# Two of four column blocks of the gates, pool output and conv output computed with the weights at rest

## The chip, the cores and the metric

One core of a Trainium2 chip runs the kernel. The metric is the device time of one execution in microseconds, lower is better. TensorE (PE) multiplies; its weight loads are shown apart as PEld. VectorE is DVE, ScalarE is ACT, GpSimd is POOL, and SyncE (SP) issues most transfers. Each engine works off its own list in the order in which the program wrote it.

## The reference

256 tokens and 16 meta tokens with 2048 features go through one layer. What the change touches:

```
u    = RMSNorm(h)
proj = u @ w_in          # z_pool 1024 | v 1024 | g 1024 | gate_a 2048 | gate_b 2048
y_a  = pool(z_pool) @ w_pool_out                  # 1024 -> 2048
y_b  = silu(LayerNorm(dwconv31(v * sigmoid(g)))) @ w_conv_out   # 1024 -> 2048
m    = sigmoid(gate_a) * y_a + sigmoid(gate_b) * y_b
h    = h + RMSNorm(m @ w_o)
...  # MLP with relu squared, 2048 -> 8192 -> 2048
```

All is float32.

## The kernel before

**Numbers.** Each float32 operand of a product is split into a high part (rounded to fp32r) and a low part (the rest), and a product is the sum of three: high by high, high by low, low by high. ScalarE makes the high part of a weight chunk (L279), VectorE subtracts it for the low part (L282).

**Chunks.** The weights come as chunks of 1 MB, 128 partitions by 2048 elements, in the order of the list `stream`. `fetch()` (L337) hands out the next chunk. Before that it opens the chunk two further on (its DMA goes to SP's queue), puts that chunk's split into the lists of ScalarE and VectorE, and calls `flush()`. There are three rooms for raw chunks and three each for high and low parts, so a split can start only when TensorE is through with the chunk three before it.

**Two ways to multiply.** `project_t` (L886) keeps a 128x128 block of the activations in the array and streams 512 columns of weights: tokens come out on the partitions, features along the row. A chunk has two token tiles, each with 12 products of 512 columns (`block_t`, L881). `project` (L558) with `mm2` keeps a 128x128 block of weights in the array and streams the 256 tokens: the weights' high part by both parts of the activations in one product of 512 columns (L540), then their low part by the activations' high part, 256 columns (L546). Features come out on the partitions, with two halves in one accumulator that have to be added. The MLP uses this form for w_up. In the stages before the gates `mm3` (L535) does each of the three products apart.

**Stages.** v, g and z_pool (to 152 us of the profile), then the two gates (b = 0 and 1, each four column blocks n of 512 with four chunks), a small map of the pool groups, the pool output (four blocks with two chunks), the conv output (four blocks with two chunks), then w_o and the MLP. A plan with due times orders w_o and the MLP; the change doesn't touch it. In the gates, pool output and conv output the order is the program's. The gates use `project_t`; ScalarE applies the sigmoid to each accumulator (L910). The pool output is multiplied into the first gate on VectorE (L947). The conv output is multiplied by the second gate and added (L996, L997) into `mts`, tokens on partitions. But w_o needs m with features on the partitions, so `feature_steps` turns each 128x512 tile with four transposes on TensorE (L978); ScalarE and VectorE split the result into `m` (L982, L985), and for n < 2 ScalarE copies it to `A` (L987), from which `sums_of_m` forms sums (L1010 to L1013). These steps wait in `after` and are written into the lists behind the first chunk of the next block.

**Work that fills in.** The depthwise convolution's taps, the pooling and the LayerNorm wait in `pending`, each with a cost. `drain(us)` (L179) adds `us` to a credit and writes steps into the lists as long as the credit pays for them. `project_t` calls it after each token tile with half of `fill` (2.9 per chunk in the gates, 2.4 in the pool output). Two marks stop a drain: FETCH, when steps in `late` aren't written yet (`flush` writes them at the next `fetch`), and LATER, which ends the call, so that what follows comes with the next call. The LayerNorm's two sums use both (L788): the adds add4 and add2 on VectorE, FETCH, the low part `cs_lo` (L801), LATER, and the sum over partitions, two products with ones on TensorE (L522):

```
return [(1.1, add4), (1.0, add2), FETCH, (0.4, low), LATER, (0, across)]
```

The first sum (cs_m) gives the mean, the second (cs_v) the variance. What the drains have not written by the end of the pool output is written there at once (`drain()`, L955).

Six PSUM banks serve as accumulators in turn; `project_t` takes two for a block.

Of the kernel before, what the change touches and what calls it, by code (L numbers as in the profile page):

```python
# [8 lines left out]
F32 = mybir.dt.float32  # L9
F32R = mybir.dt.float32r  # L10
I32 = mybir.dt.int32
AF = mybir.ActivationFunctionType
# [3 lines left out]
P = 128  # L16
CK = 4
CW = 512
# [100 lines left out]
def hybrid_block(ctx: ExitStack, tc: tile.TileContext, ins: dict, out: bass.AP):  # L119
    nc = tc.nc  # L120
    x = ins["x"][0]
    meta = ins["meta"]
    T, D = x.shape
    M = meta.shape[0]
    L = M + T
    NT = T // P
    KD = D // P
    KM = 13
    w_in = ins["w_in"][0]
# [10 lines left out]
    KP = PW // P  # L140
    KC = CC // P
# [5 lines left out]
    big = ctx.enter_context(tc.tile_pool(name="big", bufs=1))  # L147
# [7 lines left out]
    def f32(ap):  # L155
        return ap.bitcast(F32)
# [12 lines left out]
    late = []  # L169
# [33 lines left out]

    NB = D // CW
    G0 = PW + 2 * CC
# [4 lines left out]
    stream = [(w_vg[:, k:k + CK], (CK, CW)) for k in range(0, KD, CK)]  # L210
# [4 lines left out]
    for h in range(PW // HALF_CW):  # L215
        stream += columns(w_in, 0, KD, h * HALF_CW, HALF)
    standing_chunks = set()
    for n in range(2 * D // CW):
        stream += columns(w_in, 0, KD, G0 + n * CW)
    stream.append((w_grp.rearrange("g (k p) c -> p (g k) c", p=P), (NG * GD // P, GD)))  # L220
    for w, nk in ((w_pool_out, KP), (w_conv_out, KC)):
        for n in range(NB):
            stream += columns(w, 0, nk, n * CW)

    stream += columns(w_o, CK, CK, 0) + columns(w_o, 2 * CK, CK, 0)

# [122 lines left out]
    rb = const.tile([P, L], F32, name="rb")  # L349
# [89 lines left out]
    for h in range(RH):  # L439
# [5 lines left out]
    u = Tiles([big.tile([P, n, 2, -(-L // (4 * LINE)) * 4 * LINE], F32R, tag=tag,  # L445
                        name=f"u_{tag}")[:, :, :, :L] for tag, n in (("um", KM), ("ux", KD - KM))], KM)
# [111 lines left out]
    def project(act, nk, evac, name, mm=mm2, width=CW, shape=HALF, fill=0.0, ahead=2):  # L558

        ck, cw = shape  # L560
        accs = [acc[:, :width] for acc in acc_tiles(name, cw // P)]
        for kc in range(nk // ck):
            hi, lo = fetch(ahead)
            for j, acc in enumerate(accs):
                for k in range(ck):
                    kk = kc * ck + k
                    mm(acc, hi, lo, act, (k, kk), slice(j * P, (j + 1) * P), kk == 0, kk == nk - 1)
                if kc == nk // ck - 1:
                    flush(1)
                    evac(j, acc)  # L570
                if fill:
                    drain(fill * P / cw)

    def halves(acc, name):

# [210 lines left out]
    ln = {}  # L786
# [94 lines left out]
                nc.tensor.matmul(acc, act(kk)[:, a_, ts_], w_[:, k, :],  # L881
                                 start=kk == 0 and n == 0, stop=kk == nk - 1 and n == 2)

    after = []

    def project_t(act, nk, evac, name, fill=0.0):  # L886
        accs = acc_tiles(name, NT)
        for kc in range(nk // CK):
            hi, lo = fetch()
            for t, acc in enumerate(accs):  # L890
                block_t(acc, hi, lo, act, kc, nk, t)
                if kc == nk // CK - 1:
                    evac(t, acc)
                if fill:
                    drain(fill / NT)
            while after:
                after.pop(0)()


    sg = [None, None]  # L900

    def block(n):
        return slice(n * CW, (n + 1) * CW)

    def u_of(k):
        return u[:, k, :, M:]

    def evac_gate(b, n):
        def f(t, acc):
            late.append(lambda: nc.scalar.activation(sg[b][:, t, block(n)], acc, AF.Sigmoid,  # L910
                                                     scale=sc["r"][:, t:t + 1]))
        return f

    for b in range(2):
        sg[b] = big.tile([P, NT, D], F32, tag=f"s{b}", name=f"sg{b}")
# [28 lines left out]

    def evac_pool(n):
        def f(t, acc):
            nc.vector.tensor_mul(sg[0][:, t, block(n)], acc, sg[0][:, t, block(n)])  # L947
# [19 lines left out]
    pairs_room = big.tile([P, 3, 2 * T], F32, tag="ux", name="pairs")  # L967
    m = big.tile([P, LINE + KD * 2 * T], F32R, tag="um", name="m")[:, LINE:].rearrange(
        "p (k a t) -> p k a t", k=KD, a=2)

    def feature_steps(n, t, mt):

        box = {}

        def turn():
            box["pt"] = pt = misc_tile(f"mt_{n}_{t}").rearrange("p (k c) -> p k c", k=CK)
            for i in range(CK):
                nc.tensor.transpose(pt[:, i, :], mt[:, i * P:(i + 1) * P], ident)  # L978
        dst = m[:, n * CK:(n + 1) * CK, :, t * P:(t + 1) * P]

        def high():
            nc.scalar.copy(dst[:, :, 0, :], box["pt"])  # L982

        def low():
            nc.vector.tensor_sub(dst[:, :, 1, :], box["pt"], f32(dst[:, :, 0, :]))  # L985
            if n < 2:
                nc.scalar.copy(A[:, t, n], box["pt"])  # L987
        return turn, high, low

    def mt_of(n, t):  # L990
# [2 lines left out]
    def evac_conv(n):  # L993
        def f(t, acc):
            mt = mt_of(n, t)
            nc.vector.tensor_mul(mt, acc, sg[1][:, t, block(n)])  # L996
            nc.vector.tensor_add(mt, mt, sg[0][:, t, block(n)])  # L997
            blocks.extend(feature_steps(n, t, mt))
        return f

    def s_act_of(k):
        return ln["out"][:, k, :, :]


    A = big.tile([P, NT, 2, CK, P], F32, tag="a", name="A")
# [412 lines left out]
    high, low = u2_tiles(0, 1, CK, CK)  # L1418
# [56 lines left out]
    for k0 in (3 * CK, 3 * CK + 2):  # L1475
        high, low = u2_tiles(0, NT, k0, 2)
# [700 lines left out]
```

## Time and profile before

| | |
|---|---|
| time, median of 3 runs (lowest, highest) | 1179.78 us (1179.73, 1179.99) |
| profiled execution, its time | 1179.13 us |
| profiled execution, span from first to last instruction | 1177.4 us |
| busy: PE, DVE, ACT, POOL | 1167.9, 1014.5, 695.5, 123.0 us |
| granted TensorE clock, mean | 0.998 |

Rows of a group read: line, engine, operation, out<-in, shape, count, busy time, mean ns of one, and the idle time of the engine ahead of them. Rows of a timeline read: start and duration in us, engine, line, operation, and in brackets the idle time before and what ended it. Rows of the chain read: start, duration, and what was on the path that ended last. Rows by stretch give the busy time of PE, PEld, DVE, ACT and POOL with the count of instructions, then the granted clock, the DMA share and GB/s.

### The profile page before, as it was taken

The numbers are of one execution on the slowest core, as the hardware profiler recorded it, in microseconds if no ns is written. First come the engines' busy times: TensorE is split into PE (matmuls) and PEld (weight loads), VectorE is DVE, ScalarE is ACT, GpSimd is POOL, SyncE is SP. The second block draws the span as 40 slices with busy tenths as digits, with TensorE's granted clock in tenths as the row PEclk, the third lists the DMA queues.
The fourth block names the chain that finished last, engine by engine and source line by source line (L and its number), as shares of the span: only waits on it lengthen the run. The fifth ranks groups of instructions, "written<-read, shape, count | busy, mean of one in ns | idle before, by whom it ended". The sixth has DMA issues, their size and how long they took to land.

```text
span 1177.4 us, 15848 instructions
## 1 busy us (share of the span) xinstructions
PE 1167.9 (99%) x6327; PEld 1014.3 (86%) x6327; DVE 1014.5 (86%) x1111; ACT 695.5 (59%) x728; POOL 123.0 (10%) x103
## 2 busy tenths in 40 slices
PE   9999999999999999999999999999999999999997
PEld 9999988888888888898888888888888888888886
DVE  6899989986665699988997899988898978999888
ACT  6543344445753465766667666666666666676673
POOL 1133222231000001000000000000000001000000
PEclk9999999999999999999999999999999999999999
DMA  8799989999866966849899988998998898899884
GB/s 296 250 264 271 291 268 285 309 280 282 242 224 213 287 215 215 285 156 345 238 309 299 225 283 226 283 282 216 270 288 214 249 311 209 264 266 263 284 239 180
DMA packets 185419, 305.41 MB, mean 259 GB/s; under 512 B 5154, under 2 KB 93282, under 8 KB 182529
## 3 DMA queue, kind: packets, MB, share of 16 engines
q1 hardware_dynamic: 157440, 239.62, 59.2%
q0 software_dynamic: 27296, 64.12, 27.1%
q8 instruction: 50, 0.82, 0.3%
q10 hardware_dynamic: 608, 0.66, 0.2%
q14 instruction: 25, 0.20, 0.0%
HBM read 300.18 MB, written 29.36 MB: 280 GB/s over the span
## 4 chain that ended last, share of the span: by engine, by line
PE 99%; DVE 1%; DVEq 0%; issue 0%; ACT 0%; ACTq 0%
PE bank_u L540 18%; PE acc_gate L881 15%; PE bank_a L1881 11%; PE bank_u L546 9%; PE bank_b L1881 7%; PE acc_up L1881 7%; PE o_c L1228 6%; PE acc_z L535 4%; PE acc_co L881 4%; PE acc_po L881 4%; PE acc_v L535 3%; PE acc_g L535 3%; PE acc_vg L535 2%; PE acc_up L540 1%; PE bank_u L1881 1%; PE o_b L1228 1%
## 5 line engine op out<-in xcount | busy, mean ns | idle before, releaser
L540 PE MATMUL bank_u<-m,hi 128*128 128x512 f32 x960 | 330.0, 390 | 0.0
L546 PE MATMUL bank_u<-m,lo 128*128 128x256 f32 x960 | 266.1, 277 | 0.1
L279 ACT CAST hi<-raw 128x2048 fp32r<-128x2048 f32 (+2 forms) x94 | 151.2, 1620 | 183.4 <-PE acc_gate L881 46.6
L282 DVE TENSOR_TENSOR lo<-raw,hi 128x2048 fp32r<-128x2048 f32 (+2 forms) x94 | 180.0, 1924 | 60.9 <-ACT hi L279 60.4
L540 PEld LDWEIGHTS bank_u<-m,hi 128*128 128x128 f32 x960 | 180.2, 188 | 38.1
L1665 DVE TENSOR_TENSOR lo<-raw_m,hi 128x2048 fp32r<-128x2048 f32 x75 | 171.4, 2288 | 23.2 <-ACT hi L1661 23.1
L1661 ACT CAST hi<-raw_m 128x2048 fp32r<-128x2048 f32 x75 | 143.3, 1911 | 68.0 <-PE bank_u L540 32.5
L546 PEld LDWEIGHTS bank_u<-m,lo 128*128 128x128 f32 x960 | 180.5, 188 | 2.2 <-DVE lo L1665 0.5
L881 PE MATMUL acc_gate<-hi,u_um 128*128 128x512 f32 x416 | 131.2, 390 | 0.0
L601 DVE SCALAR_TENSOR_TENSOR c<-a,taps,c 128x256 f32<-128x256 f32 x240 | 98.3, 474 | 0.1
L881 PEld LDWEIGHTS acc_gate<-hi,u_um 128*128 128x128 f32 x416 | 78.2, 188 | 16.0
L881 PE MATMUL acc_gate<-lo,u_um 128*128 128x512 f32 x208 | 81.0, 390 | 0.0
L1665 DVE TENSOR_TENSOR lo<-raw_a,hi 128x2048 fp32r<-128x2048 f32 x30 | 68.6, 2288 | 9.9 <-ACT hi L1661 9.7
L334 POOL COPY rows_of<-rows_of 128x1 f32<-128x1 f32 x24 | 50.9, 2122 | 233.4 <-ACT rows_of L333 233.4
L1881 PE MATMUL bank_a<-hi,forms 128*128 128x512 f32 (+1 forms) x232 | 74.2, 383 | 0.0
L1661 ACT CAST hi<-raw_a 128x2048 fp32r<-128x2048 f32 x30 | 57.4, 1912 | 28.2 <-PE bank_u L540 8.0
L1665 DVE TENSOR_TENSOR lo<-raw_c,hi 128x2048 fp32r<-128x2048 f32 x26 | 59.5, 2288 | 10.4 <-ACT hi L1661 10.2
L1742 ACT COPY half<-bank_u 128x256 f32<-128x256 f32 x60 | 22.2, 370 | 74.0 <-PE bank_u L546 74.0
L1661 ACT CAST hi<-raw_c 128x2048 fp32r<-128x2048 f32 x26 | 49.6, 1907 | 23.9 <-PE bank_u L540 14.8
L1881 PE MATMUL acc_up<-hi,forms 128*128 128x512 f32 x184 | 60.6, 390 | 0.0
L1881 PE MATMUL bank_b<-hi,forms 128*128 128x512 f32 (+1 forms) x184 | 58.3, 380 | 0.0
L1683 POOL DMA_DIRECT2D raw_m<-in_w_down_dram x17 | 21.6, 1270 | 324.5 <-DVE fourth_pair L1665 152.3
(429 smaller groups left out, 2390.9 us busy)
## 6 DMA issues: line engine op xcount, KB each, us to landing
raw<-in_w_in_dram SPq DMA_DIRECT2D x52, 1024.0 KB, 6.2
raw_m<-in_w_down_dram SPq DMA_DIRECT2D x37, 1024.0 KB, 8.4
raw_m<-in_w_up_dram SPq DMA_DIRECT2D x33, 1024.0 KB, 6.9
sum_P<-in_w_down_dram POOLq DMA_DIRECT2D x18, 1024.0 KB, 8.8
raw_m<-in_w_down_dram POOLq DMA_DIRECT2D x17, 1024.0 KB, 9.5
raw_c<-in_w_up_dram SPq DMA_DIRECT2D x14, 1024.0 KB, 7.8
raw_a<-in_w_down_dram SPq DMA_DIRECT2D x13, 1024.0 KB, 7.2
raw_a<-in_w_up_dram SPq DMA_DIRECT2D x11, 1024.0 KB, 6.9
```

The lines of the kernel that those rows point to most:

```text
L279: nc.scalar.copy(hi[:, sl, cs], raw[:, sl, cs])
L282: nc.vector.tensor_sub(lo[:, sl, cs], raw[:, sl, cs], f32(hi[:, sl, cs]))
L334: nc.gpsimd.tensor_copy(marks[:, RH * M // 2 + a:RH * M // 2 + a + 1], marks[:, a:a + 1])
L535: nc.tensor.matmul(acc, w[:, k[0], cs], act[:, k[1], a, off:], start=first and n == 0, stop=last and n == 2)
L540: nc.tensor.matmul(acc.rearrange("p (a t) -> p a t", a=2)[:, :, ts], hi[:, k[0], cs], act[:, k[1], :, off + ts.start:off + ts.stop], start ...
L546: nc.tensor.matmul(acc[:, :T], lo[:, k[0], cs], act[:, k[1], 0, off:], start=False, stop=stop, skip_group_check=True)
L601: nc.vector.scalar_tensor_tensor(c, conv["a"][:, q, i:i + T], taps[:, q, i:i + 1], c, op0=ALU.mult, op1=ALU.add)
L881: nc.tensor.matmul(acc, act(kk)[:, a_, ts_], w_[:, k, :], start=kk == 0 and n == 0, stop=kk == nk - 1 and n == 2)
L1228: nc.tensor.matmul(acc, form(k, a_), box[w_][:, k, :], start=start and k == 0 and n == 0, stop=stop and k == CK - 1 and n == 2, skip_group ...
L1661: nc.scalar.copy(box["hi"], raw)
L1665: nc.vector.tensor_sub(box["lo"], raw, f32(box["hi"]))
L1881: nc.tensor.matmul(acc, forms[h][:, f, k, a_, :], box[w_][:, k, cs], start=start and k == 0 and n == 0, stop=stop and k == KH - 1 and n == ...
```

## The change

For the first two of the four column blocks of both gates, of the pool output and of the conv output, `project` with `mm2` takes the place of `project_t`: features come out on the partitions at once. Their chunks of weights are marked as standing (their high part gets another place inside its room). Each accumulator of 128 features is emptied by `two_parts`: ScalarE copies one half, VectorE adds the other, one column group later. A turned gate is scaled on VectorE and gets its sigmoid in one operation of 128x1024. A turned pool block multiplies each half sum into the gate. A turned conv block multiplies and adds over 128x1024 and splits straight into `m`; its sixteen transposes (two blocks, two token tiles, four each) fall away. `project` calls `drain` after each of four column groups with a quarter of `fill`, which is 2.3 per chunk in the turned gates and 1.5 in the turned pool blocks. A turned block uses four accumulators. The remaining blocks stay as they are.

```
+    TURNED = 2
...
+                if kc and after:          # in project, behind each column group
+                    after.pop(0)()
...
+    def two_parts(dst, acc, then=None):
+        nc.scalar.copy(dst, acc[:, :T])
+        def second():
+            nc.vector.tensor_add(dst, dst, acc[:, T:])
+            if then is not None:
+                then()
+        late.append(second)
...
+    def evac_gate_turned(b, n):
+        dst = turned(sg[b][:, n])
+        def scaled():
+            nc.vector.tensor_mul(dst, dst, rb[:, None, M:].broadcast_to([P, CK, T]))
+            late.append(lambda: nc.scalar.activation(dst, dst, AF.Sigmoid))
+        def f(j, acc):
+            two_parts(dst[:, j, :], acc, scaled if j == CK - 1 else None)
+        return f
...
-            project_t(u_of, KD, evac_gate(b, n), f"gate{b}{n}", fill=2.9)
+            if n < TURNED:
+                project(u, KD, evac_gate_turned(b, n), f"gate{b}{n}", shape=(CK, CW), fill=2.3)
+            else:
+                project_t(u_of, KD, evac_gate(b, n), f"gate{b}{n}", fill=2.9)
...
+    def evac_pool_turned(n):
+        def f(j, acc):
+            i = (n * CK + j) % 6
+            s = pairs_room[:, i // 2, i % 2 * T:(i % 2 + 1) * T]
+            gate = turned(sg[0][:, n])[:, j, :]
+            two_parts(s, acc, lambda: nc.vector.tensor_mul(gate, s, gate))
+        return f
...
-        project_t(y_of, KP, evac_pool(n), f"po{n}", fill=2.4)
+        if n < TURNED:
+            project(y, KP, evac_pool_turned(n), f"po{n}", shape=(CK, CW), fill=1.5)
+        else:
+            project_t(y_of, KP, evac_pool(n), f"po{n}", fill=2.4)
...
+    def evac_conv_turned(n):
+        mt = turned(mts[:, n % 2 * NT:(n % 2 + 1) * NT, :].rearrange("p a c -> p (a c)"))
+        dst = m[:, n * CK:(n + 1) * CK]
+        def merged():
+            nc.vector.tensor_mul(mt, mt, turned(sg[1][:, n]))
+            nc.vector.tensor_add(mt, mt, turned(sg[0][:, n]))
+        def high():
+            nc.scalar.copy(dst[:, :, 0, :], mt)
+        def low():
+            nc.vector.tensor_sub(dst[:, :, 1, :], mt, f32(dst[:, :, 0, :]))
+            for t in range(NT):
+                nc.scalar.copy(A[:, t, n], mt[:, :, t * P:(t + 1) * P])
+        def f(j, acc):
+            two_parts(mt[:, j, :], acc, merged if j == CK - 1 else None)
+            if j == CK - 1:
+                blocks.extend([high, low])
+        return f
...
-        project_t(s_act_of, KC, evac_conv(n), f"co{n}")
+        if n < TURNED:
+            project(ln["out"], KC, evac_conv_turned(n), f"co{n}", shape=(CK, CW))
+        else:
+            project_t(s_act_of, KC, evac_conv(n), f"co{n}")
```

More of the change, by code (lines that the diff above doesn't have):

```diff
@@ L217, in hybrid_block, with with_standing @@
     standing_chunks = set()
+    TURNED = 2
+    def with_standing(chunks, n):
+        if n < TURNED:
+            standing_chunks.update(range(len(stream), len(stream) + len(chunks)))
+        return chunks
     for n in range(2 * D // CW):
-        stream += columns(w_in, 0, KD, G0 + n * CW)
+        stream += with_standing(columns(w_in, 0, KD, G0 + n * CW), n % NB)
     stream.append((w_grp.rearrange("g (k p) c -> p (g k) c", p=P), (NG * GD // P, GD)))
@@ L572, in project @@
                     drain(fill * P / cw)
+                if kc and after:
+                    after.pop(0)()
+    after = []
     def halves(acc, name):
@@ L882, in block_t @@
                                  start=kk == 0 and n == 0, stop=kk == nk - 1 and n == 2)
-    after = []
     def project_t(act, nk, evac, name, fill=0.0):
@@ L906, in u_of, with gate_t, turned @@
         return u[:, k, :, M:]
+    def gate_t(b, n, t):
+        return sg[b][:, n, t * CW:(t + 1) * CW]
+    def turned(room):
+        return room.rearrange("p (k t) -> p k t", k=CK)
+    def two_parts(dst, acc, then=None):
[5 more added lines that the diff above has]
+        late.append(second)
     def evac_gate(b, n):
         def f(t, acc):
-            late.append(lambda: nc.scalar.activation(sg[b][:, t, block(n)], acc, AF.Sigmoid,
+            late.append(lambda: nc.scalar.activation(gate_t(b, n, t), acc, AF.Sigmoid,
                                                      scale=sc["r"][:, t:t + 1]))
         return f
+    def evac_gate_turned(b, n):
[6 more added lines that the diff above has]
+        return f
     for b in range(2):
-        sg[b] = big.tile([P, NT, D], F32, tag=f"s{b}", name=f"sg{b}")
+        sg[b] = big.tile([P, NB, NT * CW], F32, tag=f"s{b}", name=f"sg{b}")
         for n in range(NB):
-            project_t(u_of, KD, evac_gate(b, n), f"gate{b}{n}", fill=2.9)
+            if n < TURNED:
+                project(u, KD, evac_gate_turned(b, n), f"gate{b}{n}", shape=(CK, CW), fill=2.3)
+            else:
+                project_t(u_of, KD, evac_gate(b, n), f"gate{b}{n}", fill=2.9)
     y = big.tile([P, KP, 2, T], F32R, tag="k8", bufs=2, name="y")
@@ L946, in f @@
         def f(t, acc):
-            nc.vector.tensor_mul(sg[0][:, t, block(n)], acc, sg[0][:, t, block(n)])
+            nc.vector.tensor_mul(gate_t(0, n, t), acc, gate_t(0, n, t))
+        return f
+    pairs_room = big.tile([P, 3, 2 * T], F32, tag="ux", name="pairs")
+    def evac_pool_turned(n):
[4 more added lines that the diff above has]
+            two_parts(s, acc, lambda: nc.vector.tensor_mul(gate, s, gate))
         return f
```

11 lines of the change are left out of this document (5 added, 6 removed).

## The prediction

> **What bounds the kernel now.** I read the page's engine line and the sums of its chain first, then the busy times by stage, then the chain in order of time around the edited stages.
>
> ```profile
> PE 1167.9 (99%) x6327; PEld 1014.3 (86%) x6327; DVE 1014.5 (86%) x1111; ACT 695.5 (59%) x728; POOL 123.0 (10%) x103
> ...
> PE 99%; DVE 1%; DVEq 0%; issue 0%; ACT 0%; ACTq 0%
> ```
> ```profile
> 152.60:327.20 174.60, 174.60 (x775) 144.74 (x774) 139.82 (x171) 88.61 (x91) 35.73 (x28) 1.00 0.93 281
> ...
> 376.50:423.00 46.50, 46.50 (x219) 38.79 (x218) 33.92 (x33) 20.79 (x19) 4.16 (x4) 1.00 0.84 249
> ```
> ```profile
> 266.87 0.24 PE cs_m L522 x2
> 267.11 21.78 PE acc_gate L881 x96
> 288.89 0.24 PE cs_v L522 x2
> ...
> 327.24 5.75 PE acc_grp L535 x48
> ```
> ```profile
> 376.53 16.33 PE acc_co L881 x72
> 392.87 0.87 PE mt L978 x8
> 393.74 10.91 PE acc_co L881 x48
> 404.64 0.87 PE mt L978 x8
> 405.52 10.91 PE acc_co L881 x48
> 416.43 0.87 PE mt L978 x8
> 417.30 5.46 PE acc_co L881 x24
> ```
>
> TensorE is the bound: it is busy for the whole of the gates (174.60 of 174.60 us) and of the conv output (46.50 of 46.50), and 99% of the chain is PE. So whatever shortens TensorE's own list gains in full, and whatever makes TensorE wait, once, costs in full. A 512-column product takes 21.78 / 96 = 0.2269 us; a chunk of 24 takes 5.445. The cover that keeps TensorE from waiting is VectorE and ScalarE, and it isn't thick: VectorE is busy 139.82 of 174.60 us in the gates.
>
> **What goes: two pairs of turns.** The L978 rows are the transposes; eight go after conv-output block 0 and eight after block 1. Each group of eight costs 0.87 us, and the 48 products behind it take 10.91 where 48 x 0.2269 = 10.89, so 0.02 for getting going again. Gain 2 x 0.89 = **1.8 us**. Bounds: 1.74 (0.87 alone) and 1.8. The turns after block 2 and after the first step of w_o stay.
>
> **The products themselves: no change, if their pace is the fast one.** A turned chunk is 16 pairs of 512 and 256 columns with 32 weight loads; before it is 24 products of 512 with 24 loads. The MLP runs the same pairs now:
>
> ```profile
> 565.96 0.23 PE bank_u L540
> ...
> 570.86 0.23 PE bank_u L540
> ...
> 574.31 0.23 PE bank_u L540
> ...
> 580.77 0.23 PE bank_u L540
> ```
>
> From 574.31 to 580.77 are 19 pairs: 0.340 each, 16 are 5.44 us, the same as before, and the added loads hide. From 565.96 to 570.86 are 14 pairs: 0.350. So the pairs have two paces. The slow run began after a wait of TensorE for VectorE; a run that starts slow stays slow until products of 512 follow. In the small map of the pool groups (L535, 327.24) a 256-column product takes 5.75 / 48 = 0.120 where 0.340 - 0.227 = 0.113 is the fast pace, so the pool output starts behind a slow stretch. I take: slow for the four turned pool chunks (64 pairs x 0.010 = 0.64) and for the 24 pairs left of the gate block that waits (below, 0.24): **0.9 us**. Bounds: 0, and all 24 turned chunks slow, 384 x 0.010 = 3.9.
>
> **The wait that the change adds: sums over the channels.** LayerNorm's two sums are spread over TensorE's list: VectorE makes cs_lo in one drain, and the next drain call puts the two ones-products (L522) on TensorE. Between two calls lie half a chunk now (2.72 us), a quarter in a turned block (4 x 0.340 = 1.36). By adding up the credits: three turned gate blocks lie ahead, 12 chunks that give 2.3 instead of 2.9, so the sums come 7.2 us of credit, two to three chunks, later. cs_lo_m leaves chunk 0 of the second gate's block 1 (first call, products after the second call) for chunk 2 of the same block, now turned: cs_lo_m in the call after column group 0, its products in the call after group 1.
>
> ```profile
> 261.51 1.91 ACT L279 CAST hi<-raw 128x2048 fp32r<-128x2048 f32 x1 [3.18 <-issue]
> ```
> ```profile
> 263.46 2.29 DVE L282 TENSOR_TENSOR lo<-raw,hi 128x2048 fp32r<-128x2048 f32 x1 [3.19 <-ACT hi L279]
> 265.66 0.42 DVE L801 TENSOR_TENSOR cs_lo_m<-sq,cs_hi_m 128x256 fp32r<-128x256 f32 x1
> 267.14 0.42 DVE L814 TENSOR_SCALAR mean<-cs_m 128x256 f32<-128x256 f32 x1 [1.06 <-PE cs_m L522]
> ```
>
> The chunk began at 266.87 - 24 x 0.2269 = 261.42. The split of a later chunk stands first in the queues of both engines: its cast can start only when its room is free, at the chunk's start; the subtraction follows, and cs_lo_m is done at 266.08, 4.66 us into the chunk. Its products had place at 5.45, so they never waited (0.8 us to spare). In the changed kernel they have place at 2 x 1.36 = 2.72. TensorE waits 4.66 - 2.72 plus a hop: **2.0 us**. Bounds: 0 (sums fall in an unturned chunk) and 2.3.
>
> For cs_v the same adding puts cs_lo_v after the first half of chunk 1 of block 2, unturned, its products after the second half, two chunks (10.9 us) after the block began. There the queues run late. Rows for the work ahead:
>
> ```profile
> 268.92 1.07 ACT L825 ACTIVATE sq<-c 128x1024 f32<-128x1024 f32 x1
> ```
> ```profile
> 276.76 1.22 DVE L791 TENSOR_TENSOR sq<-sq 128x1024 f32<-128x1024 f32 x1
> 278.01 0.69 DVE L794 TENSOR_TENSOR sq<-sq 128x512 f32<-128x512 f32 x1
> 278.74 0.43 DVE L795 TENSOR_TENSOR sq<-sq 128x256 f32<-128x256 f32 x1
> ```
> ```profile
> L1742 ACT COPY half<-bank_u x60: 352/372/377, 540.3 to 1125.1; 128x256 f32<-128x256 f32 x60
> L1749 DVE TENSOR_TENSOR pairs<-half,bank_u x42: 412/416/422, 585.1 to 1125.5; 128x256 f32<-128x256 f32 x42
> ```
>
> Count from the start of block 1's last chunk. ScalarE casts until 1.9, VectorE subtracts until 4.1 and centres four tiles (1.25) until 5.4; ScalarE squares them until 6.4 and only then copies the last half accumulator, until 6.8. So the cast of block 2's first chunk starts 1.3 us after that block's start (5.45) and ends at 8.7; subtraction until 10.9, two late half sums (0.33 each beyond overlap) 11.6, the scaling of the turned gate (128x1024, priced as L791) 12.8, then add4 and add2 (1.25 + 0.72 + 0.43) 15.2. ScalarE runs the wide sigmoid from 12.8 to 13.9 (1.07 as L825) and holds the next cast behind it: until 15.8, subtraction 18.0, cs_lo_v 18.4. Its products' place on TensorE is 5.45 + 10.89 = 16.3. Wait **2.1 us**. Bounds: 0 (VectorE catches up) and 2.5. It comes on top of the first: nothing between the two lets TensorE catch up.
>
> **Conv output: VectorE becomes the pace.** Count from its start at 376.53.
>
> ```profile
> 399.43 1.92 ACT L279 CAST hi<-raw 128x2048 fp32r<-128x2048 f32 x1 [0.51 <-DMA raw<-in_w_conv_out_dram]
> ```
> ```profile
> 408.45 0.68 DVE L1010 TENSOR_TENSOR A<-A 128x512 f32<-128x512 f32 x1
> ...
> 411.30 2.29 DVE L282 TENSOR_TENSOR lo<-raw,hi 128x2048 fp32r<-128x2048 f32 x1
> 413.50 0.68 DVE L996 TENSOR_TENSOR mts<-acc_co,sg 128x512 f32<-128x512 f32 x1
> ...
> 414.82 0.68 DVE L996 TENSOR_TENSOR mts<-acc_co,sg 128x512 f32<-128x512 f32 x1
> 415.54 0.69 DVE L997 TENSOR_TENSOR mts<-mts,sg 128x512 f32<-128x512 f32 x1
> 416.15 2.29 DVE L282 TENSOR_TENSOR lo<-raw,hi 128x2048 fp32r<-128x2048 f32 x1
> ```
>
> Now block 2's gated tile is done at 416.23 and its turns start at 416.43: 0.2 us to spare. After the change TensorE reaches that place after seven chunks, 38.1 us instead of 39.9. VectorE does not come earlier: the cast at 399.43 waits for a weight chunk that has just landed (22.9), which the edit doesn't bring forward. From there cast 24.8, subtraction 27.0, two half sums 27.7, multiply and add over 1024 (1.25 each) 30.2, ScalarE's high part 31.3, low part 32.4, the sums of m (408.45 to 411.30: 2.85) 35.3, the next subtraction 37.5, the gating of the two token tiles (1.32 each) 38.8 and 40.1. The turns wait for the one and the other: 0.7 and 0.9, 1.6 together, less where operations that don't feed each other overlap (0.09 at each of some eight borders in the chain); I take **1.2 us**; bounds 0 and 1.8 (the whole gain). VectorE trails TensorE at the end of the stage by about as much as now, so I charge nothing in w_o.
>
> **Costed at nothing.** A turned gate block adds four half sums and one wide multiply on VectorE (4 x 0.33 + 1.25 = 2.6 us of 21.8) and puts off 4 x 0.6 = 2.4 of taps; ScalarE goes from two sigmoids of 0.68 to four copies and one of 1.07. Both hide behind splits that are due two chunks on; without that cover each late microsecond past some 6 would show. Turned pool blocks swap two multiplies of 0.69 for eight short operations, in a stage where VectorE has room. Four accumulators of six per block: column group 2 of the next block needs group 0's bank 6.8 us after it closed, and emptying takes 0.37 + 0.42. DMA issues keep their number and order; POOL's are released by ScalarE copies that come up to 4 us later, for sums used hundreds of us on.
>
> **Sum**: -1.8 + 0.9 + 2.0 + 2.1 + 1.2 = **+4.4 us**, on the profiled execution's 1179.13 us 1183.5. The median of the runs shown, 1179.78, lies 0.65 above it: I predict 1184.2.
>
> **Rivals.**
> - *VectorE and ScalarE catch up (not slower).* Place: block 2 of the second gate. If cs_lo_v is done within 10.9 us of that block's start, its wait is gone, and the sum is +2.3: 1182.1. It decides where the cast of that block's second chunk isn't held by the wide sigmoid. For it: in the present kernel cs_lo_v (287.68 with 0.42) ends 0.8 us ahead of its products. Against it: the walk above, with 2.1 to spare.
> - *No wait at all (the change does what it says).* -1.8 + 0.6: 1178.6. For it: no wait of TensorE for VectorE in these stages now. Against it: the place of cs_m's products follows from the credits alone.
> - *All pairs slow.* 384 pairs x 0.010 instead of 0.9: +3.0 more, 1187.2. For it: u's two halves aren't adjacent as the MLP's are. Against it: 512-column products behind the z stage run at full pace at once.
> - *The clock falls in the waits.*
>
> ```profile
> 1.12 3.35 PE L436 MATMUL idle<-rb 128*128 128x128 f32 x14 [1.12 <-DVE rb L350]
> ```
> ```profile
> 1169.00:1173.00 4.00, 0.11 (x1) 0.00 (x0) 3.37 (x11) 0.77 (x3) 0.00 (x0) 0.88 0.66 247
> 1173.00:1177.40 4.40, 0.00 (x0) 0.00 (x0) 0.63 (x2) 0.00 (x0) 0.00 (x0) 0.50 0.52 183
> ```
>
> TensorE's last product ends at 1169.1; the granted clock averages 0.88 over the next 3.9 us and is 0.50 after, so it held for about 3.0 us of idling. The waits that I forecast last 2.1. If they did trip it, 3.4 us at half pace (14 small products in 3.35 us at the start, 0.24 each against 0.11 for a turn) would lose 1.7 each: +3.4, 1187.6. The Trainium skill, "TensorE: Matmul & The Clock Gate", section "What's actually happening", says that a whole idle window of about 3.4 us halves the clock and a busy one restores it; by that rule these waits are too short, and the trace's 3.0 us agrees roughly.
>
> **How the numbers follow.** Forecast (both sum waits, the turn wait) 0.60; sums of v on time 0.20; no wait 0.09; all pairs slow 0.08; clock 0.03. The range 1180.4 to 1187.2 leaves out no wait, the clock, and the ends of the neighbours, some 0.18. A measurement of this kernel can tell about 0.2%, 2.4 us. Forecast, slow pairs and clock lie above it: slower 0.71. The rival with v on time and most of no wait lie within: same 0.27. The gain alone is 0.15%, so faster gets 0.02.
>
> **What would show it.** Sixteen L978 records instead of 32 before w_o. A wait of TensorE at L522 for cs_lo_m of about 2.0 us and for cs_lo_v of about 2.1; at L978 for mts of about 1.2 in all. Pair starts 0.34 apart in the gates, 0.35 in the pool output. The prediction falls if L522 doesn't wait, or if VectorE's lateness reaches the chunks themselves and TensorE waits at L540 in the turned blocks.

## The result and the profile after

| | before | after |
|---|---|---|
| time, median of 6 runs (lowest, highest) | 1179.71 us (1178.94, 1179.99) | 1186.72 us (1185.18, 1187.88) |
| profiled execution, its time and span | 1179.13, 1177.4 us | 1187.88, 1185.9 us |
| granted TensorE clock, mean | 0.998 | 0.997 |

After takes 1.0059 times as long as before, interval 1.0049 to 1.0069: 7.0 us slower, where 4.4 were forecast. The profiled execution is the longest of after's six, 8.75 us above before's.

The engine line of the page, then the waits of TensorE (us in total, times, longest):

```profile
PE 1169.7 (99%) x6503; PEld 1021.6 (86%) x6503; DVE 1029.7 (87%) x1145; ACT 704.1 (59%) x754; POOL 123.9 (10%) x103
```
```profile
PE mt L1029 <- DVE mts L1046: 2.9, 2, 2.2
PE cs_v L529 <- DVE cs_lo_v L812: 1.8, 1, 1.8
PE cs_m L529 <- DVE cs_lo_m L812: 1.8, 1, 1.8
```

The engine line says nothing: PE is busy for 99% as before, and 8 us are lost all the same. The waits name the three places that the prediction named. Two are near the size forecast (1.8 each, against 2.0 and 2.1), the third, at the turns (L1029, the old L978), is more than twice as long. Now the chain in order of time around them (start, duration, what was on the path):

```profile
274.39 2.29 DVE lo L289
276.68 0.34 DVE cs_lo_m L812
277.07 0.39 PE cs_m L529
...
296.01 2.29 DVE lo L289
298.30 0.34 DVE cs_lo_v L812
298.69 0.39 PE cs_v L529
299.08 32.76 PE acc_gate L892 x144
...
359.99 21.82 PE acc_po L892 x96
381.81 0.23 PE acc_co L547
391.45 14.45 DMA raw<-in_w_conv_out_dram
405.98 1.92 ACT hi L286
...
422.75 0.70 DVE mts L1046
423.50 0.66 PE mt L1029 x4
424.15 7.08 PE acc_co L892 x24
```

Three things are to be seen. Each LayerNorm sum is on the path behind a weight chunk's subtraction, as the walk had it. A transfer is on the path, for 14.45 us. And 24 products of the conv output take 7.08 us, where before a chunk of 24 took 5.46. Windows of 3.41 us around that chunk (busy PE, PEld, DVE, ACT, POOL, then the granted clock) show why:

```profile
420.63:424.04 3.41, 1.20 (x9) 0.96 (x10) 3.34 (x6) 0.58 (x1) 0.00 (x0) 1.00 0.61 181
424.04:427.45 3.41, 3.41 (x11) 2.67 (x10) 3.41 (x4) 2.39 (x2) 0.00 (x0) 0.50 0.33 127
427.45:430.87 3.42, 3.42 (x17) 2.79 (x16) 2.89 (x3) 0.00 (x0) 0.00 (x0) 1.00 0.00 0
```

The clock was halved for just one of these windows, behind one in which TensorE worked for 1.20 of 3.41 us.

For every kernel that follows, this table gives how much later than before TensorE started each stage (start of its first product in the profiled execution, minus the same of before), and the last product. Differences of up to some 0.9 us stand at the gates' start already, ahead of the edits.

| us later than before | gates | group map | pool out | conv out | w_o | its first o_a | last product |
|---|---|---|---|---|---|---|---|
| after | 0.11 | 4.60 | 4.60 | 5.27 | 8.48 | 8.51 | 8.45 |
| e1, sums later | 0.44 | 0.65 | 2.68 | 3.55 | 6.82 | 6.85 | 6.76 |
| e2, conv only | 0.06 | 0.06 | 0.06 | 0.06 | -0.44 | -0.41 | -0.67 |
| e3, gates and pool only | 0.39 | 6.48 | 6.47 | 7.15 | 7.18 | 7.18 | 7.14 |
| e4, sums of m later | 0.16 | 6.27 | 6.27 | 6.94 | 7.40 | 9.45 | 9.20 |
| e6, adds later | 0.53 | 6.65 | 6.65 | 7.33 | 6.82 | 9.38 | 9.72 |
| e7, credit as before | 0.86 | 3.12 | 3.11 | 3.79 | 4.99 | 4.99 | 5.03 |
| e8, turned pool last | -0.10 | 5.79 | 5.79 | 5.80 | 9.11 | 9.11 | 9.10 |
| e9, e6 to e8 together | -0.02 | 2.41 | 2.41 | 2.42 | 1.93 | 4.23 | 4.67 |
| e10, one by one | -0.10 | 0.35 | 2.39 | 4.14 | 3.62 | 3.65 | 3.78 |
| e11, e10 and e4's edit | -0.15 | 0.30 | 2.34 | 4.06 | 2.41 | 4.45 | 4.01 |
| e12, v sooner | 0.45 | 0.89 | 2.93 | 3.05 | 2.57 | 2.57 | 2.46 |
| e13, sums halved | 0.44 | 0.89 | 2.93 | 3.05 | 1.44 | 2.01 | 2.02 |

After's own row splits its 8.45 us: 4.5 in the gates (two waits and some slow pairs), 0.7 in the pool output (slow pairs), 3.2 in the conv output, which was to be the stage with the gain.

### The profile page after: what moved, and what is told of

It is laid out like the page before. It is cut to its first block, busy times and chain, and to the rows that moved or that the text cites. A ratio compares the mean times of both kernels' runs of the same rounds, so it can differ in the third digit from the quotient of the medians.

```text
span 1185.9 us, 16266 instructions
## 1 busy us (share of the span) xinstructions
PE 1169.7 (99%) x6503; PEld 1021.6 (86%) x6503; DVE 1029.7 (87%) x1145; ACT 704.1 (59%) x754; POOL 123.9 (10%) x103
## 4 chain that ended last, share of the span: by engine, by line
PE 94%; DVE 2%; DMA 2%; ACT 1%; issue 0%; SPq 0%; DVEq 0%; ACTq 0%
PE bank_u L547 18%; PE bank_a L1957 11%; PE bank_u L553 9%; PE bank_b L1957 7%; PE acc_up L1957 7%; PE acc_gate L892 6%; PE o_c L1304 6%; PE acc_gate L547 5%; PE acc_z L542 4%; PE acc_v L542 3%; PE acc_g L542 3%; PE acc_gate L553 2%; PE acc_vg L542 2%; PE acc_po L892 2%; PE acc_up L547 1%; PE acc_po L547 1%
## 5 line engine op out<-in xcount | busy, mean ns | idle before, releaser
L547 PE MATMUL acc_gate<-u_um,hi 128*128 128x512 f32 x208 | 71.7, 389 | 0.0
L892 PE MATMUL acc_gate<-hi,u_um 128*128 128x512 f32 x208 | 65.5, 389 | 0.0
L553 PE MATMUL acc_gate<-u_um,lo 128*128 128x256 f32 x208 | 57.5, 276 | 0.0
```

The costliest lines, as they stand in the source:

```text
L547: nc.tensor.matmul(acc.rearrange("p (a t) -> p a t", a=2)[:, :, ts], hi[:, k[0], cs], act[:, k[1], :, off + ts.start:off + ts.stop], start ...
L553: nc.tensor.matmul(acc[:, :T], lo[:, k[0], cs], act[:, k[1], 0, off:], start=False, stop=stop, skip_group_check=True)
L892: nc.tensor.matmul(acc, act(kk)[:, a_, ts_], w_[:, k, :], start=kk == 0 and n == 0, stop=kk == nk - 1 and n == 2)
```

## The experiments

**e1: the sums' products two calls later.**

```
-        return [..., FETCH, (0.4, low), LATER, (0, across)]
+        return [..., FETCH, (0.4, low), LATER, LATER, LATER, (0, across)]
```

> The changed kernel with two further marks that end a drain call between cs_lo and the two ones-products, for both LayerNorm sums; the same operations. Theory (the products stand on TensorE's list ahead of VectorE's work): both waits, 2.0 and 2.1 us, go, nothing takes their place, and the kernel is about 4.1 us faster than the changed one. Rival (VectorE has too much to do in the gates, and the sums are only where that shows): TensorE waits elsewhere, at a later chunk's low part or at the pool output, and at most 1 us is won.

Measured: 1185.53 us (1184.22 to 1186.79), ratio to before 1.0052, interval 1.0039 to 1.0064; 1.2 under after, with ranges that overlap, where 4.1 were expected. The waits of e1:

```profile
PE mt L1029 <- DVE mts L1046: 3.0, 2, 2.3
PE acc_po L547 <- DVE y L970: 1.9, 1, 1.9
```

Both waits for the sums are gone, and the table shows the group map only 0.65 us late. But a wait of 1.9 for y, the input of the pool output, stands in their place. Here are the rows of the LayerNorm's sigmoids in the affine steps (ScalarE; lowest, median and highest ns, start of the first and of the last), in before, after and e1:

```profile
L856 ACT ACTIVATE sq<-c,vecs x8: 586/586/593, 301.9 to 309.8; 128x256 f32<-128x256 f32 x8
```
```profile
L867 ACT ACTIVATE sq<-c,vecs x8: 585/586/590, 312.5 to 320.4; 128x256 f32<-128x256 f32 x8
```
```profile
L867 ACT ACTIVATE sq<-c,vecs x8: 585/587/594, 318.9 to 326.8; 128x256 f32<-128x256 f32 x8
```

They alternate with as many of the next line and fill ScalarE for 9 us, in e1 to 328.0. Behind them in ScalarE's list stand the casts of two weight chunks, two sigmoids of a gate and the eight high parts of y (332.62 to 335.65), with no idle time between. So the rival was right in part: a wait came up at the pool output. The marks themselves have a share in it: the steps run 6.4 us later than in after. Each mark ends a `drain` call, and `drain` keeps no more credit than the next entry costs, here 0.

**e2: the conv output turned alone; e3: the gates and the pool output turned alone.**

```
-    TURNED = 2
+    TURNED, T_GATES, T_POOL, T_CONV = 2, 0, 0, 2      # e2; e3 has 2, 2, 2, 0
...
-            if n < TURNED:        # once each at the gates, pool output, conv output and their chunks
+            if n < T_GATES:       # T_POOL, T_CONV
```

> Only the conv output's two blocks turned; gates and pool output as before (their layouts then don't match, so the numbers of the output mean nothing, the work is the same). Theory (the conv stage costs by itself: VectorE's chain behind a late weight chunk): sixteen turns less, -1.8, a wait at the remaining turns of block 2 of about 3.5 in all, and the clock at half for 3.4 us, +1.7: about +3.4 us against before, or +1.7 where the clock holds. Rival (the conv stage's wait is inherited from queues that run late since the gates): no wait here, -1.8.

> Only gates and pool output turned, conv output as before, all transposes kept (the layouts don't match, so the numbers of the output mean nothing). Theory: waits of 2.0 and 2.1 at the sums and 0.7 of slow pairs in the pool output, no wait at the turns, +4.8 us against before. Rival (the two stages share their lateness, each alone would be hidden): under +2.

Measured: e2 1179.22 us (1178.18 to 1181.37), ratio 1.0001, interval 0.9992 to 1.001, where +3.4 was expected, or +1.7 if the clock held; it held in e2's profile. e3 1186.24 us (1185.64 to 1186.64), ratio 1.0057, interval 1.0044 to 1.0071: 6.9 slower where 4.8 were expected. TensorE's wait at the turns in e2, and the products behind the wait for cs_v in e3:

```profile
PE mt L1029 <- DVE mts L1046: 0.8, 2, 0.7
```
```profile
299.36 34.35 PE acc_gate L892 x144
```

The turns' wait in e2 is 0.8 us, not the 3 of after: the turned conv output by itself isn't what makes VectorE that late. In e2 the weight chunk that block 1 needs landed 20.2 us into the stage, in after 24.1. And e3 shows that the fall of the clock doesn't belong to the conv output: 144 products that take 32.76 us in after take 34.35 here, behind the wait for cs_v. These 1.6 us are most of the 2.1 that e3 lies above its forecast.

**e4: the sums of m one block later.**

```
-        after += blocks + [sums_of_m] * (n == 2)
+        after += blocks + [sums_of_m] * (n == 3)
```

> The changed kernel with the four sums of m (2.85 us of VectorE) written one block later, behind the turns of block 2 instead of ahead of that block's gating. Theory (VectorE's chain is what the turns wait for): the tiles are ready 2.85 us earlier, the wait of 3.5 falls to under 1, the clock doesn't fall, and 3 to 4.5 us are won against the changed kernel, unless w_o's first steps then wait for VectorE (up to 1 given back). Rival (the late weight chunk alone sets the time, through ScalarE): the wait stays, under 1 us won.

Measured: 1187.87 us (1186.64 to 1188.42), ratio 1.007, interval 1.0058 to 1.0083. Nothing won. The waits at the turns in e4:

```profile
PE mt L1029 <- DVE mts L1046: 3.5, 4, 1.1
```

Two long waits have become four short ones of about the same sum (3.5 against 2.9): what block 2 no longer waits for, block 3 does. Putting these sums elsewhere in VectorE's list only moves the wait. (The clock was halved in the gates here, as in e3.)

**e6: the accumulating transfers later.** Where the conv output starts, GpSimd issues two plain transfers of 1 MB into `early_sums` and two accumulating ones onto them, for w_o. e6 puts the accumulating pair behind the first chunk of block 2:

```
+    def sums_added():
+        marks = rows_of.rearrange("p h m -> p (h m)")
...
+        nc.scalar.copy(marks[:, a:a + 1], ident[:, :1])
+        nc.gpsimd.tensor_copy(marks[:, ...], marks[:, a:a + 1])
+        sums_early(((0, 1), (1, 1)), accum_op=ALU.add)
...
-        after += blocks + [sums_of_m] * (n == 2)
+        after += blocks + [sums_of_m, sums_added] * (n == 2)
```

> The two accumulating GpSimd transfers into early_sums move from the start of the conv output to the place behind the first chunk of its block 2 (a ScalarE copy of one column, which a GpSimd copy waits for, marks the place); the two plain ones stay. Theory, the weight chunk is late because it shares the DMA engines with them: in the changed kernel the chunk issued 9.6 us into the conv output takes 14.45 us, with transfers of 5 to 8 us where nothing accumulates beside it. Then it takes under 9 us here, its cast no longer waits for it, the waits at the turns sum to under 1 us instead of 3.5, no stretch of half clock stands in the conv output, and the time is 3 to 5 us under the changed kernel's. Rival, VectorE and ScalarE are late by their own work (the longer operations over 1024 columns): the chunk lands early, yet the waits at the turns stay above 2 us and the clock still falls; under 1.5 us won. Second rival: the accumulation merely collides with the chunks behind (those of w_o), and a wait of the same size turns up in the first steps of w_o.

Measured: 1188.08 us (1186.51 to 1188.84), ratio 1.0075, interval 1.0062 to 1.0087. The chunk issued 9.6 to 9.8 us into the stage, in after and then in e6 (KB, us to landing); and e6's waits and one step of its chain:

```profile
raw<-in_w_conv_out_dram SPq DMA_DIRECT2D x1, 1024.0 KB, 14.5
```
```profile
raw<-in_w_conv_out_dram SPq DMA_DIRECT2D x1, 1024.0 KB, 6.8
```
```profile
PE o_a L1313 <- DVE m L1045: 2.4, 1, 2.4
...
PE mt L1038 <- DVE mts L1055: 0.8, 2, 0.7
```
```profile
420.79 12.46 DMA raw_o<-in_w_o_dram
```

The theory's mechanism holds: without the accumulation beside it the chunk takes 6.8 us instead of 14.5, and the turns' wait falls from 2.9 to 0.8, e2's value. How much the accumulation costs this chunk varies: beside the same two, issued at about the same place, it took 13.1 us in before and 10.5 in e2. The second rival holds too: the accumulation now lies beside a raw chunk of w_o, which takes 12.46 us, and 2.4 us of waiting come back at the first o_a step. In this run the clock was halved behind the wait for cs_v instead (144 products in 34.37 us).

**e7: as much credit as before, with e1's marks.**

```
-                project(u, ..., shape=(CK, CW), fill=2.3)
+                project(u, ..., shape=(CK, CW), fill=2.9)
-            project(y, ..., shape=(CK, CW), fill=1.5)
+            project(y, ..., shape=(CK, CW), fill=2.4)
```

> The turned blocks give as much credit as the blocks before the change (2.9 per chunk in the gates, 2.4 in the pool output, instead of 2.3 and 1.5), and two more LATER marks stand between cs_lo and its products, as in the run with the marks alone. Theory, the credit withheld is what makes the LayerNorm late: its sixteen affine operations then end before the pool output's start (about 312 instead of 328), the wait of 1.9 us for y at the pool output goes, and neither sum is waited for; the waits at the turns and the fall of the clock there stay. Time about 4 us under the changed kernel's, 1182.5. Rival, VectorE cannot carry the turned blocks' added sums beside as many taps: TensorE waits for VectorE at the products of the turned gate blocks (the low part of a chunk) by more than 1 us, and under 2 us are won.

Measured: 1184.28 us (1183.64 to 1184.42), ratio 1.0042, interval 1.0029 to 1.0054: 2.4 under after's median, not 4. Its waits, and its row of the LayerNorm:

```profile
PE mt L1029 <- DVE mts L1046: 2.5, 2, 1.8
PE cs_m L529 <- DVE cs_lo_m L812: 1.4, 1, 1.4
```
```profile
L867 ACT ACTIVATE sq<-c,vecs x8: 586/588/590, 311.0 to 318.9; 128x256 f32<-128x256 f32 x8
```

As expected the affine steps are 8 us earlier than in e1, the wait for y is gone, and the turns' wait stays. Not as expected, cs_m is waited for again: with more credit its first call falls earlier in the turned block, and three calls a quarter of a chunk apart (4 us) are too short. No clock fell in this execution, and no turned gate block waited for a chunk's low part, so the rival has nothing for it.

**e8: the turned pool blocks last.**

```
-    for n in range(NB):
+    for n in (2, 3, 0, 1):       # in the list of chunks for w_pool_out, and around the pool output
```

> The pool output computes its blocks in the order 2, 3, 0, 1, so that the turned ones come behind products of 512 columns and not behind the small map's 256-column ones. Theory, a run of pairs that starts behind 512-column products is fast: the 64 pairs of the pool output stand 0.340 us apart instead of 0.350 and the stage is 0.65 us shorter; time 0.6 us under the changed kernel's. Rival, the pace belongs to the stage (its operand y, or the engines' load): the pairs stay at 0.350 and nothing is won.

Measured: 1187.01 us (1185.5 to 1188.76), ratio 1.0067, interval 1.0053 to 1.008. Its chain around the pool output, and two windows in the gates:

```profile
360.56 0.23 PE acc_po L547
```
```profile
382.34 0.23 PE acc_co L547
```
```profile
274.67:278.08 3.41, 1.65 (x10) 1.28 (x10) 2.90 (x4) 0.00 (x0) 0.00 (x0) 1.00 0.97 368
278.08:281.49 3.41, 3.41 (x13) 2.93 (x12) 0.89 (x1) 0.07 (x1) 0.00 (x0) 0.50 1.02 398
```

The 64 pairs take 382.34 - 360.56 = 21.78 us, 0.340 each; in after they took 359.99 - 337.59 = 22.40, 0.350 each. The pace follows what ran before, as the theory has it, and the stage is as short as before the change (0.01 in the table). The time doesn't show it, since the clock fell twice in this execution, in the gates behind the wait for cs_m and once more in the conv output.

**e9: the three edits together.**

> The three edits of the other runs of this call together: accumulating transfers later, credit as before with the two marks, pool blocks in the order 2, 3, 0, 1. Theory, the waits and the clock are all that stands between the change and its gain: no wait of TensorE over 0.5 us from the gates to the conv output, no stretch of half clock, pairs at 0.340; the gain of the turns (1.8) is left, and the time is 1177.5 to 1179, 0.5 to 1.8 under the kernel before. Rival, lateness of VectorE and ScalarE moves on with each edit: a wait of over 1 us stands somewhere behind, in w_o or at the turns, and the time stays at 1181 or above.

Measured: 1183.93 us (1183.38 to 1185.19), ratio 1.0043, interval 1.003 to 1.0055; the theory's 1177.5 to 1179 is missed by 4.9 or more, the rival's "over 1 us in w_o" is right. Its waits:

```profile
PE o_a L1313 <- DVE m L1045: 2.1, 1, 2.1
PE cs_m L529 <- DVE cs_lo_m L812: 1.4, 1, 1.4
```

Each is a wait known from e6 or e7; at the turns 0.8 is left, as in e6. The conv output alone is 0.5 us shorter than before's (2.42 to 1.93 in the table).

**e10: one accumulation at a time, cs_m five calls later.** To e9:

```
-        ... (0.4, low), LATER, LATER, LATER, (0, across)]
+        ... (0.4, low)] + [LATER] * (5 if key == "m" else 3) + [(0, across)]
-        after += blocks + [sums_of_m, sums_added] * (n == 2)
+        after += [lambda e=n - 1: sums_added(e)] * (n in (1, 2)) + blocks + [sums_of_m] * (n == 2)
```

**e11** is e10 with e4's edit.

> As the run of the three edits together, with two more: the two accumulating transfers start one at a time, the first behind the first column group of the second chunk of the conv output's block 1, the second behind the first chunk of block 2; and five LATER marks stand between cs_lo_m and its products (three for cs_v). Theory, each wait that was left has its own cause and goes with it: one accumulation alone slows the chunk beside it to under 9 us, so the raw chunk of w_o no longer takes 12.2 us and the wait of 2.1 at the first o_a step goes; the wait for cs_lo_m (1.4) goes, and with it the slow pairs behind it (about 0.4). Left are the turns' wait (0.8) against the gain of 1.8: 1179.3 to 1180.3, level with the kernel before. Rival, the sum of what VectorE and ScalarE have to do in the turned blocks is too large, and a wait of over 1 us shows at another place from the gates to w_o: 1181.5 or more.

> The same with the four sums of m (L1083 to L1086, 2.85 us of VectorE) a block later, behind the turns of block 3. Theory, they are what makes the gating of block 2 late by 0.8 now that the weight chunk is on time: the wait at these turns goes, none of the same size comes, and the time is 0.5 to 0.9 us under the other run of this call, 1178.5 to 1179.5. Rival, as with this edit alone: they hold up the gating of block 3 instead, its turns wait 1 to 2 us, and the time is equal or higher.

Measured: e10 1183.14 us (1181.76 to 1183.47), ratio 1.0029, interval 1.0018 to 1.004; e11 1182.81 us (1182.49 to 1183.77), ratio 1.0029, interval 1.0018 to 1.0039. e10's longest wait, its LayerNorm row, two windows at the pool output, and the start of the pairs behind cs_m's products in its chain:

```profile
PE acc_po L892 <- DVE y L970: 1.9, 1, 1.9
```
```profile
L867 ACT ACTIVATE sq<-c,vecs x8: 585/587/594, 318.6 to 326.5; 128x256 f32<-128x256 f32 x8
```
```profile
332.67:336.09 3.42, 1.54 (x10) 1.20 (x9) 3.42 (x5) 3.42 (x9) 0.00 (x0) 1.00 0.89 294
336.09:339.50 3.41, 3.41 (x10) 2.67 (x9) 3.41 (x6) 1.07 (x1) 0.00 (x0) 0.50 0.90 320
```
```profile
269.54 0.23 PE cs_m L529 x2
269.78 0.23 PE acc_gate L547
270.13 0.23 PE acc_gate L547
```

The waits for cs_m and at o_a are gone, and the group map is 0.35 us late: the turned gates cost next to nothing then. But the five calls put the affine steps back to where e1 had them, the wait for y is back, and with it a half clock. So the rival came true, at e1's place. e11 has the same at the pool output, and at the turns 1.7 in two waits instead of 0.8: its rival too.

**e12: two marks instead of three for cs_v. e13: the same, with two of the four sums of m a block later.**

```
-        ... [LATER] * (5 if key == "m" else 3)
+        ... [LATER] * (5 if key == "m" else 2)
...
+    def more_sums_of_m():         # e13: L1085 and L1086 move here from sums_of_m
...
-        ... blocks + [sums_of_m] * (n == 2)
+        ... blocks + [sums_of_m] * (n == 2) + [more_sums_of_m] * (n == 3)
```

> As the run with the accumulations one at a time, but two LATER marks instead of three between cs_lo_v and its products. In that run cs_lo_v was ready at 295.9 and its products stood at 300.1; a call earlier they have place at 297.4. Theory, the LayerNorm's affine steps ran on ScalarE until 327.7 because cs_v came late, held back the splits and so y, and cost the wait of 1.9 at the pool output and the half clock after it (1.7): with cs_v a call earlier they end before 320, that wait and the fall go, and no wait over 0.9 us is left from the gates to w_o: 1179.0 to 1180.0. Rival, the wait for y has another cause (the casts of the first pool chunks): it stays above 1.5 us and the time above 1182.

> The same with the last two of the four sums of m (L1085, L1086, 1.4 us) a block later and the first two where they were. Theory, VectorE gates block 2 then 1.4 us sooner and block 3 1.4 us later, which the 0.2 to 1.1 us of room on both sides carry: the waits at the turns fall from 0.8 to under 0.5 in sum, and the time is 0.3 to 0.8 us under the other run of this call, the first version with a gain, 1178.5 to 1179.2. Rival, what is taken from block 2 is added at block 3: the sum of the waits stays at 0.8 or more and the two runs are level.

Measured: e12 1182.51 us (1181.87 to 1183.43), ratio 1.0025, interval 1.0016 to 1.0034; e13 1182.24 us (1181.1 to 1182.81), ratio 1.0021, interval 1.0012 to 1.0029. e13's waits, the LayerNorm row of e12, and the window around e12's wait for y:

```profile
PE acc_po L892 <- DVE y L970: 1.9, 1, 1.9
...
PE mt L1038 <- DVE mts L1055: 0.4, 1, 0.4
```
```profile
L867 ACT ACTIVATE sq<-c,vecs x8: 585/587/594, 319.1 to 327.0; 128x256 f32<-128x256 f32 x8
```
```profile
334.11:337.52 3.41, 1.76 (x8) 1.47 (x9) 3.41 (x7) 3.41 (x6) 0.00 (x0) 1.00 1.00 339
```

e12's theory fell, and its rival's numbers came: the products of cs_v came 2.2 us earlier than in e10, but the affine steps didn't move, so what holds them at 319 isn't that place of cs_v's products. The traces show what is in between, the square root of the variance on ScalarE, in e10 and then in e12:

```profile
303.42 0.42 ACT L846 ACTIVATE ln_q<-ln_var 128x256 f32<-128x256 f32 x1
```
```profile
304.24 0.42 ACT L846 ACTIVATE ln_q<-ln_var 128x256 f32<-128x256 f32 x1
```

It came no sooner (e12's gates began 0.55 us later). The program puts it into `late`, with a FETCH mark behind it, so it is written at the next `fetch`. A call earlier still lies in the same chunk (5.4 us, two calls), before the same `fetch`, and all that follows stays. That the wait for y comes from the late affine steps rests on two groups: with the last sigmoid starting at 326 to 327 (e1, e10 to e13) it was 1.9 each time, with it at 318 to 319 (e7, e9) there was none. In e13 the waits at the turns fell to 0.4, as its theory had it, but the two times can't be told apart. Of the versions with all three stages turned e13 comes nearest to the kernel before, and still lies above it; none beats it.

## Why the prediction was right, and where it wasn't

It named the direction, the places of the three waits and their makers; the size was 2.5 us short at the median. That the time still lies below the forecast's upper end, 1187.2, is luck: that end came from the rival of slow pairs, and what took up the room was the turns' wait and the clock.

- *Turns.* Right: 16 records are left, and in e2 the conv output is 0.5 us shorter; the other 1.3 of the 1.8 are lost around its remaining turns, where the waits' row has 0.8.
- *The waits for the sums, 2.0 and 2.1.* Right, as the waits and the chain show; the walk of both queues against the place of the products gave them. The rival with v on time and the one with no wait are out.
- *The pace of the pairs, 0.9.* Right in size: 0.62 in the pool output by the stretch above, the rest in the gates, where the first blocks ran at 0.340. The reason was only half right: a wait isn't needed. In e10 the pairs behind the two 256-column products of cs_m stand 0.35 apart, and no wait lies there.
- *The wait at the turns, 1.2.* Wrong, and this is the term that was mis-sized: the waits' row has 2.9, and the stage's account leaves 3.3 (3.2 later, of which 1.6 is the clock, with 1.7 won by the turns). The step that failed is "a weight chunk that has just landed (22.9), which the edit doesn't bring forward". It landed later, 24.1 us into the stage, and from there the walk is right: cast at 24.2 instead of 22.9 adds 1.3 to everything behind it. The walk's 1.6 and this 1.3 make the row's 2.9, so the 0.4 that the sum took off for overlap didn't come either. The quoted rows of before showed that the cast waited 0.51 for this transfer; a term that hangs on a transfer without slack needed a bound for a later landing, and "the whole gain" was none. e6 shows what stretches the transfer, the accumulating transfers beside it. Why the accumulation costs the chunk more in after (14.5) than in before (13.1) and in e2 (10.5, with the same stage), stays open.
- *The clock.* Given 0.03 and left out of the sum; it fell. Its price was right: a halved window behind the turns cost 7.08 - 5.45 = 1.6 us, and 34.35 - 32.76 = 1.6 in e3. The rule behind the small chance was wrong. The 3.0 us of idling at the kernel's end, and the Trainium skill ("TensorE: Matmul & The Clock Gate", section "What's actually happening": a whole idle window of about 3.4 us halves the clock), both speak for a wait longer than these. Here waits of 2 us did it, inside a window in which TensorE still worked for 1.2 to 1.65 of 3.41 us.
- *Costed at nothing.* Right as far as it went: in no run does TensorE wait for a chunk in a turned gate block. The credit withheld put the LayerNorm's affine steps off: in after they run from 312.5, 10.6 us later than before. That alone cost nothing. In e1, e10 and e12 TensorE gets y 8.7 us behind the start of the last sigmoid; by an estimate from these, after's last, at 320.4, gives y at 329.1, ahead even of the 332.8 at which TensorE starts the pool output in before. The wait for y came with the marks of e1, which put the steps off by another 6.4 us.

So the change loses by lateness, and each cure uncovered or made the next lateness: cs_m, y, the weight chunk, w_o's chunk. With all that was found (e13) 2.9 us remain, of which the wait for y is 1.9.

## What to carry to other kernels

A gain of 1.8 us in an engine that is 99% busy is worth only what the engines feeding it have to spare: before taking time out of the bound, list for each operand how early it is ready now (here 0.2 us at the turns, 0.8 at each sum, less than nothing at the chunk), since a wait costs in full and may halve the clock on top. A schedule by credits moves other work when blocks give less credit, or a mark drops it, so follow the deferred work to its own user. When a cure removes a wait without winning its time, look for the same microseconds one stage on before giving up the mechanism.

## What the runs showed of the hardware

- *Half clock after part of an idle window.* All falls between the gates and w_o lasted 3.413 us and began at the end of a stretch of the same length, on one grid per run, in which TensorE had been idle for more than half. After a busy time of 1.20, 1.54 and 1.65 us of 3.41 the clock fell (the windows of after, e10 and e8). With 1.56 in e7 and 1.62 in e9 (the first two rows below), with 1.65 in another window of after (the last two rows) and with 1.76 in e12, whose wait of 1.9 was cut by a boundary, it didn't. So a wait near 2 us is at the edge and how it lies on the grid counts, but the busy time of the window alone doesn't decide; what else does stays open. The Trainium skill, in the section named above, says that the window is free-running, and these falls agree.

```profile
416.94:420.35 3.41, 1.56 (x8) 0.98 (x7) 3.38 (x4) 0.32 (x1) 0.00 (x0) 1.00 0.18 10
```
```profile
432.14:435.55 3.41, 1.62 (x8) 1.00 (x6) 3.41 (x4) 3.41 (x7) 0.00 (x0) 1.00 1.05 402
```
```profile
273.86:277.27 3.41, 1.65 (x10) 1.29 (x9) 3.12 (x4) 0.90 (x2) 0.25 (x1) 1.00 0.79 250
277.27:280.69 3.42, 3.42 (x21) 3.00 (x21) 1.65 (x2) 0.48 (x1) 0.00 (x0) 1.00 1.04 410
```

- *Two paces of the same pair of products.* 0.340 us behind products of 512 columns, 0.350 behind 256-column ones, and a run keeps its pace (e8 against after).
- *Accumulating transfers.* 1 MB of weights took 6.8 us without two accumulations beside it (e6) and 10.5, 13.1 and 14.5 us with them (e2, before, after); another chunk, beside which they were moved, took 12.46.
